# A hybrid decoder step on one core: keys and values of the last two heads as two pairs in seven products

## The chip, the cores and the metric

The kernel runs on one core of a Trainium2 chip. The metric is the device time of one execution in microseconds (us). Five engines work side by side, each through its own list of instructions in a fixed order: TensorE (PE in the profile; its weight loads are PEld), VectorE (DVE), ScalarE (ACT), GpSimd (POOL) and SyncE (SP), which here only issues DMAs. An instruction that waits for another engine holds up everything behind it in its own list. L269 is line 269 of the kernel.

## The reference, cut to what matters

One layer of a decoder: 16 meta tokens and 512 prompt tokens (causal) and 8 sequences of 4 new tokens each, which read a paged cache of 512 earlier positions (4 pages of 128 rows per sequence). Together 560 token columns; 8 heads of 128; model width 2048. Everything is float32.

```python
h = rmsnorm(x, g_pre)
q, k, v, ga, cb, cc, ch, gc, ma, mc = split(h @ w_in)
a = stick_breaking(q, k, v) * silu(ga)      # prompt: over its own rows; new tokens: pages, then their own rows
c = cb * causal_conv3(cc * ch) * silu(gc)
m = sigmoid(ma + b_ga) * (a @ w_pa) + sigmoid(mc + b_gc) * (c @ w_pc)
y = x + rmsnorm(m @ w_out, g_post)

def stick_breaking(q, k, v):
    z = q @ k.T * HEAD_DIM ** -0.5 + b_sb
    log_keep = where(mask, log_sigmoid(-z), 0)
    after = cumsum(log_keep, reverse) - log_keep
    return where(mask, exp(log_sigmoid(z) + after), 0) @ v
```

The outputs are the new rows of the prompt and of the 8 sequences, and the new keys, values and convolution rows.

## The kernel before, in words

**Products in split float32.** Each operand x is kept as a rounded part hi and the rest lo = x − hi. A product is three TensorE matmuls, hi·hi, hi·lo and lo·hi. The normalised input, turned so that its 2048 features lie in 16 blocks of 128 rows, stays in memory as `h_hi` and `h_lo`, 560 columns each, used as two halves of 280 (`HC`). Weights arrive from SP's DMA as pieces of 1024 rows by 128 columns (`w_load`, tile `raw`); `w_split` makes `whi` by a copy on ACT (L253) and `wlo` by a subtraction on DVE (L254).

**Two ways of making a projection.** `gemm` (L261 to L276, matmuls at L269) takes 128 columns of the weight at a time: 16 blocks × 3 matmuls × 2 halves = 96 matmuls of 280 columns. `pair` (L1044) takes 256 columns at once and cuts weight and input into 2 × 2 blocks; `seven` (L999) forms the result from seven block products instead of eight, each 8 × 3 = 24 matmuls (`product`, L994), 168 for two column tiles. For this, sums of input blocks T1, T2, T3 are needed (`t_hi0` to `t_lo2`, parts hi and lo), a fourth difference r1 that replaces one block of the input, and sums `s` of weight blocks.

**The stages.** First the normalisation, with the queries of heads 0 to 3 made as its columns come (`q_chunk`), and `q_proj` for these: scale, store, and a 128x32 transpose of the 32 decode columns per head. Then for each of heads 0 to 3 `head_now`: keys by `gemm` (`k_proj`), values by `gemm` (`v_proj`), the query of head 4 + h by `gemm`, and the stick-breaking attention of the prompt (`attend`; scores at L634, sums at L716, the product with the values at L728). Then `head_later` for heads 4 to 7: keys and values by `gemm`, turned by transposes (`natural`, L519 to L523), stored for later. Then all remaining projections by `pair`, then attention of heads 4 to 7, and the output products.

**The decode part** runs between these as a chain of small steps (`decode_steps`). A step of its first half takes one page of keys and makes 16 dot products of 128 elements on DVE (L795); there are 64 such pages. Calls of `dec_step` say how many steps stand at a place: in `head_now` and `head_later` 24 pages (`DEC1` = 6 units of 4) are worked, the other 40 by `dec_group`, one call per group of gate products.

**The block sums** T1 to T3 and r1 (lines 951 to 981) stand in the program behind `head_later`, two of eight feature blocks at a time, on 274 of the 280 columns: nine DVE operations, three ACT copies (L956) and three DVE subtractions (L957) for each of four rounds, and four more splits that put r1 into the input's block.

**The order.** Within an engine the order is a scheduler's, by priorities that follow the program's text, so work that stands later may fill gaps; an instruction put through `keep_in_program_order` (`pin`) stays in the order in which it was written against others so marked.

## Time and profile before

| what | us |
|---|---|
| median of 3 runs (lowest, highest) | 1575.22 (1573.78, 1578.06) |
| the profiled execution | 1577.82 |
| its span on the core | 1576.2 |
| PE busy in the span | 1561.8 |
| DVE busy | 1260.8 |
| ACT busy | 755.6 |

The mean granted TensorE clock of the profiled execution is 0.998 of full speed. The end of head 3's attention lies at 295 us of the span, the first matmul of a `pair` at 369.6.

In the profile a row of a group reads: line, engine, operation, output tile <- input tiles, count, busy time, mean time of one, idle time before and who ended it. A row of the timeline reads: start, duration, engine, line, operation, and in brackets the idle time just before on that engine and what ended it. Durations of pipelined instructions overlap, so what one costs when rows stand close is the distance of two starts. A window's row gives the stretch, its length, and the busy time of PE, PEld, DVE, ACT and POOL in it (instructions in brackets), then the granted TensorE clock, the DMA engines' share and GB/s.

### The profile page before, as it was taken

To read this page: it belongs to the slowest core of one execution; us is meant where nothing else is said; L and a number is where in the kernel's file an instruction comes from. 1 tells how busy PE (TensorE), PEld (TensorE's weight loads), DVE (VectorE), ACT (ScalarE), POOL (GpSimd) and SP (SyncE) were. 2 spreads that over 40 slices of the span, in tenths; PEclk is the share of its full clock that TensorE was granted. 3 is DMA by queue.
4 is the path that set the end of the run, shared out by engine and by line. 5 is a ranking of instruction groups with operands and counts; after the bars stand their busy time and mean duration, and the time that the engine had idled before them with its cause. 6 is when DMAs were issued, how large, how long until landed. Compare 5 with 4: busy or idle time off the path is not lost.

```text
span 1576.2 us, 32345 instructions
## 1 busy us (share of the span) xinstructions
PE 1561.8 (99%) x12172; PEld 1528.3 (97%) x12172; DVE 1260.8 (80%) x3567; ACT 755.6 (48%) x1345; POOL 236.3 (15%) x428
## 2 busy tenths in 40 slices
PE   9999999999999999999999999999999999999997
PEld 8999999999999999999999999898899999999997
DVE  6328999965799999999999996655678867877776
ACT  6335555434444443444444465444476734355563
POOL 1023333222011001011011113212100010000000
PEclk9999999999999999999999999999999999999999
DMA  8245655344563454545356547666596455433345
GB/s 250 73 143 175 178 165 178 117 125 130 170 189 113 144 153 143 149 135 162 106 173 187 157 143 224 185 207 219 166 292 188 140 186 167 153 107 95 101 140 189
DMA packets 300674, 252.77 MB, mean 160 GB/s; under 512 B 11521, under 2 KB 268613, under 8 KB 299701
## 3 DMA queue, kind: packets, MB, share of 16 engines
q1 hardware_dynamic: 272021, 160.45, 34.8%
q0 software_dynamic: 28368, 89.98, 17.2%
q8 instruction: 95, 1.56, 0.4%
q14 instruction: 62, 0.51, 0.1%
q10 hardware_dynamic: 128, 0.27, 0.1%
HBM read 217.95 MB, written 32.71 MB: 159 GB/s over the span
## 4 chain that ended last, share of the span: by engine, by line
PE 98%; DVE 1%; ACT 0%; issue 0%; DVEq 0%; ACTq 0%
PE mm L994 34%; PE mm L269 28%; PE o L994 25%; PE mm L334 2%; PE z L716 1%; PE o L728 1%; PE z L334 1%; PE tp L870 1%; PE z L634 1%; PE tp L519 0%; PE z L1332 0%; PE mm L187 0%; PE tp L169 0%; DVE x_n L1374 0%; PE z L227 0%; DVE hn L220 0%
## 5 line engine op out<-in xcount | busy, mean ns | idle before, releaser
L253 ACT CAST whi<-raw 128x1024 fp32r<-128x1024 f32 x247 | 259.3, 1051 | 323.1 <-PE mm L269 100.3
L254 DVE TENSOR_TENSOR wlo<-raw,whi 128x1024 fp32r<-128x1024 f32 x247 | 301.8, 1223 | 105.5 <-ACT whi L253 103.4
L994 PE MATMUL mm<-h_hi,whi 128*128 128x272 f32 (+1 forms) x1152 | 333.0, 289 | 0.0
L994 PE MATMUL mm<-h_lo,whi 128*128 128x272 f32 (+1 forms) x1152 | 332.7, 289 | 0.0
L994 PE MATMUL mm<-h_hi,wlo 128*128 128x272 f32 (+1 forms) x1152 | 331.7, 290 | 0.1
L994 PE MATMUL o<-t_hi,whi 128*128 128x272 f32 (+1 forms) x864 | 250.2, 290 | 0.0
L994 PE MATMUL o<-t_lo,whi 128*128 128x272 f32 (+1 forms) x864 | 249.9, 289 | 0.0
L994 PE MATMUL o<-t_hi,wlo 128*128 128x272 f32 (+1 forms) x864 | 249.8, 289 | 0.0
L795 DVE CUSTOM_DVE_ANT_0 junk<-kpage,qb 128x128 f32<-128x128 f32 x1024 | 245.3, 286 | 2.1 <-DMA qb<-q_scr 1.6
L994 PEld LDWEIGHTS mm<-h_hi,whi 128*128 128x128 f32 x1152 | 217.4, 189 | 6.7 <-ACT whi L253 3.4
L994 PEld LDWEIGHTS mm<-h_hi,wlo 128*128 128x128 f32 x1152 | 216.6, 189 | 1.3 <-DVE wlo L254 0.5
L994 PEld LDWEIGHTS mm<-h_lo,whi 128*128 128x128 f32 x1152 | 216.8, 188 | 0.1
L253 ACT CAST whi<-s 128x1024 fp32r<-128x1024 f32 x126 | 132.1, 1048 | 150.1 <-PE mm L994 54.2
L254 DVE TENSOR_TENSOR wlo<-s,whi 128x1024 fp32r<-128x1024 f32 x126 | 153.8, 1220 | 61.1 <-ACT whi L253 60.9
L269 PE MATMUL mm<-h_lo,whi 128*128 128x280 f32 (+1 forms) x640 | 187.6, 293 | 0.0
L269 PE MATMUL mm<-h_hi,wlo 128*128 128x280 f32 (+1 forms) x640 | 187.1, 293 | 0.0
L269 PE MATMUL mm<-h_hi,whi 128*128 128x280 f32 (+1 forms) x640 | 186.7, 292 | 0.0
L994 PEld LDWEIGHTS o<-t_hi,wlo 128*128 128x128 f32 x864 | 163.1, 189 | 0.7 <-DVE wlo L254 0.7
L994 PEld LDWEIGHTS o<-t_lo,whi 128*128 128x128 f32 x864 | 163.4, 189 | 0.0
L994 PEld LDWEIGHTS o<-t_hi,whi 128*128 128x128 f32 x864 | 163.0, 189 | 0.1
L269 PEld LDWEIGHTS mm<-h_lo,whi 128*128 128x128 f32 x640 | 120.3, 188 | 0.8
L269 PEld LDWEIGHTS mm<-h_hi,whi 128*128 128x128 f32 x640 | 120.5, 188 | 0.5
(462 smaller groups left out, 3166.7 us busy)
## 6 DMA issues: line engine op xcount, KB each, us to landing
raw<-in_w_in SPq DMA_DIRECT2D x192, 512.0 KB, 4.2
kpage<-in_cache_k POOLq DMA_DIRECT2D x64, 256.0 KB, 3.6
qb<-q_scr POOLq DMA_DIRECT2D x32, 512.0 KB, 5.7
vpage<-in_cache_v POOLq DMA_DIRECT2D x64, 256.0 KB, 5.9
raw<-in_w_out SPq DMA_DIRECT2D x32, 512.0 KB, 3.9
gate_scr<-g POOLq DMA_DIRECT2D x32, 272.0 KB, 3.3
gt<-gate_scr POOLq DMA_DIRECT2D x16, 544.0 KB, 4.6
raw<-in_w_pc SPq DMA_DIRECT2D x16, 512.0 KB, 4.5
```

Of the source, the lines that this page charges most:

```text
L253: act.copy(hi, x)
L254: low[0] = dve.tensor_sub(lo, x, hi.bitcast(F32))
L269: pe.matmul(o, lhsT=w, rhs=r[:, t0:t1], start=(k == 0 and n == 0), stop=(k == nk - 1 and n == 2))
L334: pin(pe.matmul(o, lhsT=l, rhs=r[:, k, t0:t1], start=(start and m == 0), stop=(stop and m == 2), skip_group_check=True))
L634: pe.matmul(zt[:m, c0:c0 + n], lhsT=l[:, s0:s0 + m], rhs=r[:, ts:ts + n], start=(c0 == 0 and i == 0), stop=(i == 2), skip_group_check=True)
L716: pe.matmul(o, lhsT=l, rhs=x, start=False, stop=(i == len(ops) - 1), skip_group_check=True)
L728: pe.matmul(ot[:, ts - NMETA:ts - NMETA + n], lhsT=l[:m, st, :], rhs=x[:m, c0:c0 + n], start=False, stop=(g == GROUPS[-1] and i == 2), ski ...
L795: dve.tensor_tensor_reduce(out=junk, in0=kt[:, h * P:(h + 1) * P], in1=qt[:, t, h * P:(h + 1) * P], scale=1.0, scalar=0.0, op0=ALU.mult, o ...
L870: pin(pe.matmul(po[32 * j:32 * (j + 1), :], lhsT=lhs, rhs=rhs, start=(pg == 0), stop=last and n >= len(vts) - 4, tile_position=(0, 32 * j) ...
L994: pe.matmul(o, lhsT=l[:, k, :], rhs=r, start=(start and k == 0 and m == 0), stop=(stop and k == 7 and m == 2), skip_group_check=True)
```

## The change

It has three parts.

1. **Keys and values of heads 6 and 7** are made by `pair`, keys of both heads in one pair and values in another (`later_pair`). Heads 4 and 5 stay with `gemm`: four column tiles, now written as a loop in which the block sums stand by hand between the tiles (`STEPS`). The first pair's weight pieces and its first sum `s` are loaded and formed within the last of these four tiles (`ready`).
2. **The block sums** cover all 280 columns and are written in two steps of two feature blocks each: `t_sums` (six DVE operations) and `t_parts` (two DVE operations, three ACT copies, three DVE subtractions). They are pinned, and so are the `wlo` of the four tiles. The copies of 16 and 32 rows in `natural` move from DVE to ACT for heads 4 and 5.
3. **The first decode queries.** The decode columns of heads 0 to 3 are turned by one 128x128 transpose, copied once and stored by four DMAs together, ahead of the loads of the small tables. `PAGES` sets the steps: one page before head 0, then 19 in heads 0 to 3, so that 20 pages are worked there (`DEC1` = 5) and 44 by `dec_group`. The decode queries of heads 6 and 7 are read back from memory for their `z_new`.

```diff
-DEC1 = 6
+DEC1 = 5
+SOLO = 6
-    def w_split(x):
+    def w_split(x, pin=lambda ins: ins):
...
-        low[0] = dve.tensor_sub(lo, x, hi.bitcast(F32))
+        low[0] = pin(dve.tensor_sub(lo, x, hi.bitcast(F32)))
...
-    def natural(raw, nat, nat_s):
+    def natural(raw, nat, nat_s, copy=dve.tensor_copy):
...
+        if h < FIRST:
+            act.activation(qs_all[:, h, :], ob[:, PQ - HQ:], AF.Copy, scale=SCALE)
         pool.dma_start(qt_scr[h][:, q0:], qr[:, q0:])
+        if h < FIRST:
+            return
...
+    PAGES = ((2, 2, 2, 1), (1, 1, 2, 1), (1, 1, 1, 1), (1, 1, 1, 0))
...
         khi, klo = k_split(np_, k_proj(h))
-        dec_step(1 if h else 0, "part")
-        vhi, vlo = v_proj(h, np_)
-        dec_step(1, "part")
+        dec_step(PAGES[h][0], "part")
+        vhi, vlo = v_split(np_, v_proj(h))
+        dec_step(PAGES[h][1], "part")
         q_proj(NOW + h)
-        dec_step(2, "part")
+        dec_step(PAGES[h][2], "part")
         ot = next(attend(np_, h, khi, klo, vhi, vlo, *q_split(np_, qr)))
-        dec_step(2, "part")
-        at = np_.tile([P, PQ], F32, name="at", bufs=1)
+        dec_step(PAGES[h][3], "part")
+        at = hp.tile([P, TQ], F32, name="qr", bufs=2)[:, 0:PQ]
...
-    def head_later(h):
-        pool.dma_start(k_scr[h], k_proj(h))
-        dec_step(2, "part")
-        v_proj(h)
-        dec_step(2, "part")
+    def later_pair(c, h, qs=None, ready=None):
+
+        raws = [hp2.tile([P, T], F32, name="raw", bufs=2) for _ in range(2)]
+        seen = []
+        for m, half, b in pair(c + h * P, HC, ready):
+            act.copy(raws[m][:, NMETA + half * HQ:NMETA + (half + 1) * HQ], b[:, HM:])
+            act.copy(raws[m][:, half * HM:(half + 1) * HM], b[:, :HM])
...
-        if n <= 25:
+        if n <= 27:
...
-            dec_step(2 if n in (26, 28) else 1)
+            dec_step(2 if n <= 30 else 1)
+    for h in range(FIRST):
+        q_proj(h)
+    pt = t_ps()
+    pe.transpose(out=pt[:, 0:P], in_=qs_all[:, 0:FIRST, :].rearrange("p h t -> p (h t)"), identity=ident)
+    qn = hp.tile([P, P], F32, name="qn4", bufs=1)
+    act.copy(qn, pt[:, 0:P])
+    for h in range(FIRST):
+        pool.dma_start(q_scr[:, h * P:(h + 1) * P], qn[h * TS:(h + 1) * TS])
...
+    dec_step(1, "part")
...
-    for h in range(NOW, H):
-        head_later(h)
...
+        def whole(out, c, *ij):
+            pin(dve.tensor_add(out, part(h_f, c, *ij), part(l_f, c, *ij)))
+        def t_sums(c):
+
+            x, y = held[c] = [tsp.tile([P, 2, HC], F32, name=n) for n in "xy"]
+            r = part(r1, c)
+            whole(y, c, 0, 0)
+            whole(r, c, 0, 1)
+            pin(dve.tensor_sub(r, y, r))
+            whole(x, c, 1, 1)
+            pin(dve.tensor_add(x, r, x))
+            pin(dve.tensor_sub(y, y, x))
+        def t_parts(c):
+
+            x, y = held.pop(c)
+            t_split(part(t_hi[0], c), part(t_lo[0], c), x)
+            z = tsp.tile([P, 2, HC], F32, name="z", bufs=1)
+            whole(z, c, 1, 0)
+            t_split(part(t_hi[1], c), part(t_lo[1], c), y)
+            pin(dve.tensor_sub(z, z, x))
+            t_split(part(t_hi[2], c), part(t_lo[2], c), z)
+        tiles = [c + h * P for h in range(NOW, SOLO) for c in (GATE_K, GATE_V)]
...
+        units = {(0, u): unit(0, u) for u in range(2)}
+        STEPS = (((t_sums, 0),), ((t_sums, 2), (t_parts, 0)), ((t_parts, 2), (t_sums, 4), (t_parts, 4)),
+                 ((t_sums, 6), (t_parts, 6)))
+        for i in range(len(tiles)):
+            h = NOW + i // 2
+            if i:
+                units[i, 1] = unit(i, 1, pin)
+            o = gemm([units[i, u] for u in range(2)], h_rhs, ALL)
+            if i + 1 == len(tiles):
+                first_ws = blocks_of(win, GATE_K + SOLO * P)
+            for step, c in STEPS[i]:
+                step(c)
+            if i + 1 < len(tiles):
+                units[i + 1, 0] = unit(i + 1, 0, pin)
+            else:
+                pin(dve.tensor_add(first_sum, first_ws[1], first_ws[2]))
+                for c in range(0, 8, 2):
+                    t_split(blk(h_hi, 0, 1)[:, c:c + 2], blk(h_lo, 0, 1)[:, c:c + 2], r1[:, c:c + 2])
+            raw = raw_of(o)
+            if i % 2 == 0:
+                k_store(h, raw)
+                k_out(hp, h, raw, qs_all[:, h, :], act.copy)
+            else:
+                v_store(h, v_out(hp, h, raw, act.copy))
...
-    def seven(ws, n, rb, rt, s, tmp, sums=None):
+    def seven(ws, n, rb, rt, s, tmp, sums=None, summed=False):
...
+        later_pair(GATE_K, SOLO, qs, (first_ws, first_sum))
+        later_pair(GATE_V, SOLO)
```

Behind the pairs the program is as before, but for the tile `after`, which is made a little later from another pool.

Three places show how the change moves the rows. Line numbers of the kernel before and of the changed one differ by a few: the `gemm` matmul is L269 before and L270 now, the values' product of `attend` L728 and L722, `natural`'s transposes L519 to L523 and L501 to L505, the casts of T L956 and L992, the subtractions behind them L957 and L993.

The first place is TensorE at the end of head 3's attention (its output is `o_3998` before, `o_3939` now). Before, `mm_4471` is the keys of head 5 in `gemm`, and `tp_4442`, `tp_4448` are the transposes of head 4's values:

```order
L728 MATMUL o_3998<-hiA_4049,vhi_3652 128x512
L519 MATMUL tp_4442<-ident_73,raw_4435 128x128 x4
L269 MATMUL mm_4471<-h_hi_89,wlo_4468 128x280
...
L728 MATMUL o_3998<-loA_4050,vhi_3652 128x512
L728 MATMUL o_3998<-hiA_4049,vlo_3653 128x512
L269 MATMUL mm_4471<-h_lo_90,whi_4467 128x280
...
L269 MATMUL mm_4472<-h_hi_89,whi_4461 128x280
L522 MATMUL tp_4448<-ident_73,raw_4435 16x128
L523 MATMUL tp_4448<-ident_73,raw_4435 32x128
```

Now, with `tp_4308` and `tp_4314` the transposes of head 4's values, `mm_4331` the keys of head 5 and `mm_4492` its values:

```order
L722 MATMUL o_3939<-hiA_3990,vhi_3640 128x512
L722 MATMUL o_3939<-loA_3991,vhi_3640 128x512
L722 MATMUL o_3939<-hiA_3990,vlo_3641 128x512
L501 MATMUL tp_4308<-ident_73,raw_4301 128x128 x4
L270 MATMUL mm_4492<-h_hi_89,whi_4457 128x280
L270 MATMUL mm_4492<-h_lo_90,whi_4457 128x280
L504 MATMUL tp_4314<-ident_73,raw_4301 16x128
L505 MATMUL tp_4314<-ident_73,raw_4301 32x128
L270 MATMUL mm_4331<-h_hi_89,wlo_4298 128x280
L270 MATMUL mm_4331<-h_hi_89,whi_4297 128x280
```

Between the four large transposes of head 4's values and the two small ones, which use the same buffer, 25 matmuls stood; now two stand there.

The second place is ScalarE at the same point. `at_4142` before and `qr_3997` now is the copy of head 3's attention output. Before:

```order
L520 COPY nat_4440<-tp_4442 128x512
L745 COPY at_4142<-o_3998 128x512
L579 COPY raw_4569<-mm_4471 128x272
L579 COPY raw_4569<-mm_4471 128x8
L253 CAST whi_4602<-raw_4600 128x1024
...
L956 CAST t_hi0_5269<-x_5285 128x548
```

Now:

```order
L741 COPY qr_3997<-o_3939 128x512
L992 CAST t_hi0_4005<-x_4135 128x560
L992 CAST t_hi1_4010<-y_4136 128x560
L992 CAST t_hi0_4005<-x_4278 128x560
L992 CAST t_hi1_4010<-y_4279 128x560
L502 COPY nat_4306<-tp_4308 128x512
L506 COPY nat_4306<-tp_4314 16x128
L992 CAST t_hi2_4015<-z_4288 128x560
```

The copy `nat` that empties the buffer of head 4's large transposes stood ahead of the attention output's copy; now it stands behind that copy and four casts of the block sums.

The third place is VectorE behind the last operation of head 3's attention (`loA`). Now, with `wlo_4298` and `wlo_4328` the low parts of the weights of head 5's keys:

```order
L491 TENSOR_TENSOR loA_3991<-eA_3987,hiA_3990 128x512
L993 TENSOR_TENSOR t_lo0_4006<-x_4135,t_hi0_4005 128x560
L1007 TENSOR_TENSOR z_4288<-h_hi_89,h_lo_90 128x560
L993 TENSOR_TENSOR t_lo1_4011<-y_4136,t_hi1_4010 128x560
L1027 TENSOR_TENSOR z_4288<-z_4288,x_4135 128x560
L993 TENSOR_TENSOR t_lo2_4016<-z_4288,t_hi2_4015 128x560
L255 TENSOR_TENSOR wlo_4298<-raw_4295,whi_4297 128x1024
L255 TENSOR_TENSOR wlo_4328<-raw_4325,whi_4327 128x1024
```

Before, the block sums stood among the weights of later heads, mostly one at a time:

```order
L254 TENSOR_TENSOR wlo_4603<-raw_4600,whi_4602 128x1024
L968 TENSOR_TENSOR r1_5284<-r1_5284,h_lo_90 128x548
L969 TENSOR_TENSOR x_5285<-r1_5284,h_hi_89 128x548
L969 TENSOR_TENSOR x_5302<-r1_5284,h_hi_89 128x548
L254 TENSOR_TENSOR wlo_4731<-raw_4728,whi_4730 128x1024
L970 TENSOR_TENSOR x_5285<-x_5285,h_lo_90 128x548
```

The subtraction that makes the weights' low part for the next tile now has the five rows of `t_parts` ahead of it; before, it had one or two rows of the sums between it and the next. From `t_lo0_4006` to the low part of the first pair's sum `s`, 36 rows of 560 elements and 8 of 1024 stand on VectorE.

More of the change, by code (lines that the diff above doesn't have):

```diff
@@ L523, in natural @@
         pe.transpose(out=pt[0:TS, P:2 * P], in_=raw[:, TP:T], identity=ident)
-        dve.tensor_copy(nat[0:16, 4, :], pt[0:16, 0:P])
-        dve.tensor_copy(nat_s, pt[0:TS, P:2 * P])
+        copy(nat[0:16, 4, :], pt[0:16, 0:P])
+        copy(nat_s, pt[0:TS, P:2 * P])
     BLK = {}
@@ L933, in hybrid_step_kernel @@
     for h in range(NOW):
-        q_proj(h)
-    for h in range(NOW):
         head_now(h)
     nctx.close()
-    for h in range(NOW, H):
-        head_later(h)
     dec_step(64, "part")
@@ L947, in hybrid_step_kernel, with blocks_of @@
         ttp = tctx.enter_context(tc.tile_pool(name=f"tt{i}", bufs=1))
-        t_hi.append(ttp.tile([P, 8, HU], F32R, name=f"t_hi{i}"))
-        t_lo.append(ttp.tile([P, 8, HU], F32R, name=f"t_lo{i}"))
+        t_hi.append(ttp.tile([P, 8, HC], F32R, name=f"t_hi{i}"))
+        t_lo.append(ttp.tile([P, 8, HC], F32R, name=f"t_lo{i}"))
+    def blocks_of(src, c):
+        c1, c2, k1, k2 = slice(c, c + P), slice(c + P, c + 2 * P), slice(0, 1024), slice(1024, 2048)
+        return [w_load(src[k, m]) for k, m in ((k1, c1), (k1, c2), (k2, c2), (k2, c1))]
@@ L978, in hybrid_step_kernel, with part @@
-        for c in range(0, 8, 2):
-            t_split(blk(h_hi, 0, 1)[:, c:c + 2], blk(h_lo, 0, 1)[:, c:c + 2], r1[:, c:c + 2])
+        r1 = tsp.tile([P, 8, HC], F32, name="r1", bufs=1)
+        first_sum = sp2.tile([P, 8, P], F32, name="s")
+        held = {}
+        def part(x, c, *ij):
+            return (blk(x, *ij) if ij else x)[:, c:c + 2]
+        def whole(out, c, *ij):
[9 more added lines that the diff above has]
+            pin(dve.tensor_sub(y, y, x))
@@ L1011, in seven @@
         product(x, w_split(w11), rb(0, 0), True, False)
-        with behind(last):
-            dve.tensor_add(s, w21, w22)
+        if not summed:
+            with behind(last):
+                dve.tensor_add(s, w21, w22)
         product(q, w_split(s), rb(0, 1), True, False)
@@ L1037, in seven, with pair @@
         yield 1, 0, y
-    def blocks_of(src, c):
-        c1, c2, k1, k2 = slice(c, c + P), slice(c + P, c + 2 * P), slice(0, 1024), slice(1024, 2048)
-        return [w_load(src[k, m]) for k, m in ((k1, c1), (k1, c2), (k2, c2), (k2, c1))]
-    def pair(c, n):
+    def pair(c, n, ready=None):
         hs = [(HC - n, HC), (T - n, T)]
@@ L1051, in rt @@
         def rt(i):
-            return lambda k: (t_hi[i][:, k, HU - n:HU], t_lo[i][:, k, HU - n:HU])
-        ws = blocks_of(win, c)
-        s = sp2.tile([P, 8, P], F32, name="s")
-        yield from seven(ws, n, rb, rt, s, lambda name: sp2.tile([P, HU], F32, name=name)[:, :n])
-    gctx, uctx = ExitStack(), ExitStack()
-    sp2 = gctx.enter_context(tc.tile_pool(name="sums", bufs=1))
+            return lambda k: (t_hi[i][:, k, HC - n:], t_lo[i][:, k, HC - n:])
+        ws, s = ready or (blocks_of(win, c), sp2.tile([P, 8, P], F32, name="s"))
+        yield from seven(ws, n, rb, rt, s, lambda name: sp2.tile([P, HC], F32, name=name)[:, :n], summed=ready is not None)
+    with tc.tile_pool(name="heads2", bufs=1) as hp2:
+        qs = hp2.tile([P, H - SOLO, TS], F32, name="qs")
+        for h in range(SOLO, H):
+            pool.dma_start(qs[:, h - SOLO, :], qt_scr[h][:, PQ:TQ])
+        later_pair(GATE_K, SOLO, qs, (first_ws, first_sum))
+        later_pair(GATE_V, SOLO)
     gp = gctx.enter_context(tc.tile_pool(name="gates", bufs=2))
@@ L1163, in hybrid_step_kernel @@
             if j + w == 14:
-                after = hl[0].tile([P, P], F32, name="after")
-                dve.tensor_scalar_add(after, neg_u.bitcast(F32), 1.0)
                 loaded = head_loads(NOW, hl[0])
@@ L1170, in hybrid_step_kernel @@
     hs0 = hlctx.enter_context(tc.tile_pool(name="split0", bufs=1, side="right"))
+    after = hs0.tile([P, P], F32, name="after")
+    dve.tensor_scalar_add(after, neg_u.bitcast(F32), 1.0)
     def head_split(pl, x):
```

108 lines of the change are left out of this document (53 added, 55 removed).

## The prediction

> **What bounds the kernel now.** I read the page's first part, then the chain of waits, then TensorE's waits.
>
> ```profile
> PE 1561.8 (99%) x12172; PEld 1528.3 (97%) x12172; DVE 1260.8 (80%) x3567; ACT 755.6 (48%) x1345; POOL 236.3 (15%) x428
> PE 98%; DVE 1%; ACT 0%; issue 0%; DVEq 0%; ACTq 0%
> PE o L227 <- DVE hn L220: 2.0, 2, 1.3
> PE tp L169 <- DVE neg_one L114: 1.4, 1, 1.4
> PE z L227 <- DVE hn L220: 0.5, 1, 0.5
> ```
>
> TensorE is busy for 99% of the span and is 98% of the chain. The three waits, 3.9 us together, are the only ones that the view of TensorE's waits gives, and they belong to the normalisation. So a matmul less is time less, and any wait that the change brings to TensorE is time more: there is no slack of TensorE that could absorb it. The windows by stage (length, then PE, PEld, DVE, ACT and POOL busy) show how near the other engines are:
>
> ```profile
> 42.00:93.00 51.00, 51.00 (x392) 50.23 (x391) 14.25 (x24) 15.41 (x31) 8.21 (x15) 1.00 0.32 96
> 93.00:271.00 178.00, 178.00 (x1367) 173.61 (x1366) 152.39 (x799) 93.82 (x190) 59.19 (x110) 1.00 0.56 168
> 271.00:370.00 99.00, 99.00 (x766) 97.07 (x766) 75.17 (x216) 40.27 (x82) 23.33 (x43) 1.00 0.39 116
> 455.00:945.00 490.00, 489.94 (x3860) 487.70 (x3860) 474.13 (x1591) 225.16 (x336) 54.42 (x90) 1.00 0.50 149
> 945.00:1164.00 219.00, 219.00 (x1735) 202.53 (x1734) 133.89 (x152) 101.53 (x145) 46.61 (x85) 1.00 0.66 208
> ```
>
> From 93 us to 271 us (heads 0 to 2 and most of 3) VectorE is at 86%, and TensorE still never waits. From 271 to 370, where the keys and values of heads 4 to 7 and all block sums lie, it is at 76%: the sums cost TensorE nothing, because eight column tiles of 96 matmuls cover them.
>
> **What is removed.** Four column tiles of 96 matmuls become two pairs of 168: 384 − 336 = 48 matmuls of 280 columns less. One costs, from the chain:
>
> ```profile
> 168.99 8.99 PE mm L269 x70
> 369.63 3.03 PE mm L994 x24
> 92.77 0.27 PE L552 MATMUL tp<-ident,qr 128*32 128x128 f32 x1
> 92.80 0.38 PE L269 MATMUL mm<-h_lo,whi 128*128 128x280 f32 x1
> 93.02 0.29 PE L269 MATMUL mm<-h_hi,wlo 128*128 128x280 f32 x1
> ```
>
> 8.99 / 70 = 0.128 us (a `product` of 272 to 280 columns: 3.03 / 24 = 0.126). 48 × 0.1285 = **6.2 us**. Four turned queries become one: the turn sets the next matmul off by 0.03 and that one lasts 0.09 longer than usual (0.22 to its successor), 0.12 each, so three fewer give 0.35. Together **−6.5 us**. The Trainium skill ("TensorE: Matmul & The Clock Gate", section "Wait — 56ns, not 53.3ns?") gives a warm matmul its columns at 2.4 GHz and 2.5 ns, 119 ns for 280, which would make the 48 worth 5.7 us; the row here measures 128 ns, and it decides.
>
> **What the cover loses.** The block sums now have four column tiles to hide behind, and the second product of the first pair has its weights' low part on VectorE behind all of them. I work this out from s, the start of head 3's last attention matmul.
>
> ```profile
> 295.35 0.40 PE L728 MATMUL o<-hiA,vlo 128*128 128x512 f32 x1
> 295.78 0.59 ACT L745 COPY at<-o 128x512 f32<-128x512 f32 x1 [1.29 <-PE o L728]
> 308.01 0.59 ACT L520 COPY nat<-tp 128x512 f32<-128x512 f32 x1 [3.14 <-PE tp L519]
> 308.49 0.28 ACT L587 ACTIVATE z_new<-z,bsb 32x32 f32<-32x32 f32 x1
> 308.68 1.18 ACT L956 CAST t_hi<-x 128x548 fp32r<-128x548 f32 x2
> 323.93 0.66 ACT L956 CAST t_hi<-x 128x548 fp32r<-128x548 f32 x1
> 269.69 0.40 PE L716 MATMUL z<-hiA,neg_u 128*128 128x512 f32 x1
> 269.92 0.29 PE L269 MATMUL mm<-h_lo,whi 128*128 128x280 f32 x1
> 275.77 0.60 PE L519 MATMUL tp<-ident,raw 128*128 128x128 f32 x4
> 276.13 0.38 PE L269 MATMUL mm<-h_hi,whi 128*128 128x280 f32 x1
> ```
>
> *First stall.* The small transposes of head 4's values share a buffer with the large ones and wait for its copy `nat`. In the new order that copy stands on ScalarE behind the attention output's copy and four casts. The output's copy starts at s + 0.43 (295.35 to 295.78) and holds ScalarE for 0.48 (308.01 to 308.49); casts follow each other at 1.18 − 0.66 = 0.52, call it 0.53 for 560 columns; `nat` takes 0.59 and its signal 0.04: 0.43 + 0.48 + 4 × 0.53 + 0.59 + 0.04 = 3.66. TensorE has until then the last attention matmul (269.69 to 269.92, 0.23), four transposes (0.36) and two matmuls (0.26): 0.85. It waits **2.8 us**. Before, 25 matmuls (3.2 us) stood at that place.
>
> *Second stall.* Directly behind these transposes stands the first matmul with the low weights of head 5's keys. That subtraction is pinned on VectorE behind the five rows of `t_parts`.
>
> ```profile
> 309.34 0.73 DVE L957 TENSOR_TENSOR t_lo<-x,t_hi 128x548 fp32r<-128x548 f32 x1 [0.60 <-ACT t_hi L956]
> 309.99 0.72 DVE L973 TENSOR_TENSOR y<-y,h_lo 128x548 f32<-128x548 f32 x1
> 310.63 0.72 DVE L957 TENSOR_TENSOR t_lo<-x,t_hi 128x548 fp32r<-128x548 f32 x1
> 336.07 0.73 DVE L957 TENSOR_TENSOR t_lo<-x,t_hi 128x548 fp32r<-128x548 f32 x1 [0.86 <-ACT t_hi L956]
> 301.93 1.21 DVE L254 TENSOR_TENSOR wlo<-raw,whi 128x1024 fp32r<-128x1024 f32 x1
> 303.06 0.71 DVE L968 TENSOR_TENSOR r<-r,h_lo 128x548 f32<-128x548 f32 x1
> 122.67 0.43 DVE L486 TENSOR_SCALAR loA<-eA 128x512 f32<-128x512 f32 x1 [1.38 <-ACT eA L481]
> 123.14 0.69 DVE L487 TENSOR_TENSOR loA<-eA,loA 128x512 f32<-128x512 f32 x1
> ```
>
> Short rows follow each other at 0.64 (309.99 to 310.63), a long one holds VectorE for 1.13 (301.93 to 303.06). The fifth row, t_lo2, needs the cast of z, which stands behind `nat` and the small copy, thus behind the first stall: cast from about s + 4.2 to 4.9, t_lo2 0.64, the long row 1.25 to its end, about s + 6.8. TensorE is there at 3.66 + 0.24 = 3.9. It waits **2.9 us**.
>
> *The whole stretch.* From t_lo0 to the low part of the pair's sum s, which the third matmul of the pair's second product needs, VectorE has 36 short and 8 long rows (the order above). It starts at s + 0.43 + 0.48 + 0.66 + 0.03 = s + 1.6; 36 × 0.64 + 7 × 1.13 + 1.25 = 32.2; in each of four `t_parts` it waits for the last cast, 0.86 as in the row at 336.07, 3.4 together: s + 37.2. TensorE needs 214 matmuls × 0.1285 = 27.5, the attention matmul 0.23 and some 2.6 of transposes: s + 30.3. So it loses at least **6.9 us**, of which the two stalls are 5.7 and the rest falls at the start of values 5 and of the pair. Some rows need the row right ahead (r = y − r, x = r + x, y − x, z − x): there the successor starts only after the full duration and 0.04 (122.67 + 0.43, then 123.14). With 12 such rows at 0.12 it is 8.3. With every row at its full 0.72 or 1.22 (40.7) it is 10.4. I take **8.7**, nearest to the dependent count with a little for the signals between engines; bounds 6.9 to 10.4. Below 6.9 it could come only if VectorE's rows ran closer than the row at 309.99 shows.
>
> **Early decode steps.** By the new order 25 dot products lie inside head 0's sums where 6 lay before.
>
> ```profile
> 125.89 0.29 DVE L795 CUSTOM_DVE_ANT_0 junk<-kpage,qb 128x128 f32<-128x128 f32 x1
> 126.10 0.29 DVE L795 CUSTOM_DVE_ANT_0 junk<-kpage,qb 128x128 f32<-128x128 f32 x1
> ```
>
> At 0.21 each, 19 more are 4.0 us of VectorE ahead of what TensorE needs. Heads 1 to 3 have had as many before and TensorE waited for none, so most of it is covered by the matmuls of the next query: bounds 0 to 4.0, I take **0.6**. Four stores and the tables' loads change places in POOL's queue in a stretch in which POOL is busy 8.21 of 51 us (the window from 42 us); what waits for them (the bias in `z_new`, the first page) stands behind head 0's keys, a dozen us of matmuls. I cost them at nothing; a late bias would hold ScalarE's next weight copy and TensorE behind it.
>
> **At nothing.** The four pages that move to `dec_group` are 4 × 16 × 0.21 = 13.4 us of VectorE. Calls per group are unchanged up to the 25th group, so the stretch from 455 us, where VectorE is at 474.13 of 490, keeps its density; the pages land where it is busy 133.89 of 219. Without that room each would cost up to 3.4. The weights of the pairs are as many pieces as those of four tiles, so SP's queue is as long; the two small reloads of queries are wanted only at the end of a pair.
>
> **The sum**, against the profiled execution (1577.82 with a span of 1576.2): −6.5 + 8.7 + 0.6 = **+2.8 us**, 1580.6 for such an execution. The median of the runs shown is 1575.22, 2.6 lower, so there: **1578.0 us**. What a measurement of this kernel can tell from no change is about 0.3%, 4.7 us: the forecast is no change, on the slow side.
>
> **Rivals.**
>
> *The saving stays.* The waits are absorbed and 6.5 us, or nearly, remain: 1568.7. For it: 271 to 370 us had the same sums at 75.17 of 99 and no wait. Against: that took eight tiles, and the ledger leaves 37 us of VectorE beside 30 of TensorE. Chance 0.15.
>
> *Head 0 waits too.* The sums of head 0 stand, by the new order, behind 51 dot products in all, and TensorE pays the whole 4.0: −6.5 + 8.7 + 4.0 = +6.2, 1581.4, slower. It decides once VectorE reaches head 0's sums later than TensorE has run through the next query's 96 matmuls (12.3 us). For it: VectorE is at 86% there. Against: heads 1 to 3. Chance 0.20.
>
> *The clock drops.* After two stalls with 0.24 us of work between them TensorE may be granted half its clock. At the start of the span ten wide matmuls run slow:
>
> ```profile
> 1.36 4.63 PE tp L169 x10
> ```
>
> 0.46 each against 0.23 at 269.69, and full speed after 4.6 us; that again costs half, 2.3 us: +5.1, 1580.3. Chance 0.10. The Trainium skill ("TensorE: Matmul & The Clock Gate", section "What's actually happening") lets the clock halve after an idle window of about 3.4 us, in windows that run freely; the stalls of 2.8 and 2.9 would each stay under it, and by that rule the drop mostly does not come.
>
> **How the numbers follow.** The forecast has 0.55; its own range is 1574.5 to 1581 (stretch 6.9 to 10.4 and head 0 at 0 to 1 give 1575.6 to 1580.1, and 1 us to each side for the scatter of the median). The range reaches to the head 0 rival with the stretch at 10.4 in part, 1584, and toward the saving to 1571, which leaves out most of the first rival and a little at the top: **1571.0 to 1584.0**. Slower by over 0.3% is above 1579.9: 0.12 of the forecast, 0.18 of head 0, 0.05 of the clock, **0.35**. Faster, under 1570.5: **0.13**. Within: **0.52**.
>
> **What would show it.** TensorE's waits should name `nat` (2.8) and `wlo` (2.9) behind head 3's attention, then shorter ones up to the pair, 7 to 10 us in all, in a stretch where VectorE is close to full. The first matmul of the keys' pair of heads 6 and 7 and all later stages should keep their old lengths. No waits there, waits in the gate products, a granted clock below 1.00, or a head 0 with more than 1 us of waits would each make a term wrong.

## The result and the profile after

The changed kernel takes 1585.55 us (median of 4 runs, 1585.03 to 1586.16) against 1574.57 us of the kernel before beside it (4 runs, 1573.78 to 1578.06): a ratio of 1.0067, 95% interval 1.0054 to 1.0079. It is 0.67% or 11 us slower. The prediction had 1578.0 us, no change, and a range that ends at 1584.0.

The first part of the changed kernel's page:

```profile
span 1583.4 us, 32270 instructions
PE 1554.8 (98%) x12121; PEld 1520.3 (96%) x12121; DVE 1269.7 (80%) x3569; ACT 763.1 (48%) x1366; POOL 245.0 (15%) x430
```

TensorE is busy 7.0 us less than before (1561.8), and the span is 7.2 us longer. The 7.0 is not the 48 matmuls alone: 5.3 of it lies ahead of the first `gemm` matmul, where executions differ anyway, and matmuls at half clock, seen below, count as busy for longer. The view of TensorE's waits (who waits, for whom, us in total, times, longest) has new rows besides those of the normalisation:

```profile
PE mm L270 <- DVE wlo L255: 4.5, 2, 2.8
PE tp L504 <- ACT nat L502: 3.1, 2, 2.7
PE z L710 <- ACT hiA L490: 1.8, 1, 1.8
PE z L574 <- ACT raw L564: 1.0, 1, 1.0
PE mm L1073 <- DVE wlo L255: 0.7, 1, 0.7
PE tp L876 <- DMA vpage<-in_cache_v: 0.7, 1, 0.7
```

And the windows by stage (columns as in the prediction):

```profile
93.00:271.00 178.00, 174.20 (x1320) 169.56 (x1319) 149.71 (x790) 92.04 (x179) 63.45 (x103) 0.99 0.48 152
271.00:370.00 99.00, 91.34 (x674) 88.22 (x673) 68.07 (x89) 46.35 (x95) 22.08 (x41) 0.97 0.37 111
455.00:945.00 490.00, 489.92 (x3874) 488.18 (x3872) 474.01 (x1634) 216.28 (x322) 55.04 (x95) 1.00 0.51 153
```

The loss lies in the first two windows: TensorE is idle for 3.8 us in heads 0 to 3 and for 7.7 us in the stretch after them, and the granted clock is under 1.00 in both. The third window stands as before, although four pages more now lie behind it.

Spans of single executions are not directly comparable here: the first `gemm` matmul starts at 78.4 us in the profile of before and at 74.7 us in that of after, in a part that the change does not touch (e10 below, with the changed beginning, starts there at 78.15). So I measure from that matmul. To the first matmul of the convolution's first pair it takes 291.1 us before and 301.0 us after, **+9.95**; from there to the last product of `seven` 1183.9 and 1184.4, and in every experiment 1183.0 to 1184.5. Nearly all of the change lies in the first piece. I cut it again at s, the start of head 3's last attention matmul, and take 0.1285 us off for each `gemm` or `seven` matmul in between, since orders differ in how many stand on which side. What is left, "net", is the other matmuls, every wait and what half clock costs:

| kernel | heads 0 to 3, net | s to third matmul of the pair's second product, net | first gemm to convolution |
|---|---|---|---|
| before | 39.5 | – | 291.1 |
| after | 44.3 | 13.8 | 301.0 |
| e1 late steps | 39.7 | 13.7 | 296.4 |
| e2 registers behind | 43.7 | 13.7 | 300.3 |
| e3 units ahead | 47.5 | 12.8 | 304.3 |
| e4 no pair | 46.6 | – | 298.6 |
| e5 unpinned, late | 39.4 | 1.6 | 286.6 |
| e6 one pair, late | 38.9 | 3.8 | 286.6 |
| e7 lows on POOL, late | 42.7 | 16.3 | 303.2 |
| e8 wait filled, late | 39.6 | 12.2 | 294.9 |
| e9 unpinned, early | 47.4 | 1.7 | 293.1 |
| e10 four query tiles | 38.7 | 12.7 | 294.3 |
| e11 e10 and unpinned | 39.0 | 1.7 | 284.8 |
| e12 e5, four query tiles | 39.2 | 1.6 | 286.4 |

The 12.2 us of e8 hold 6.1 us of matmuls that it adds. Without any wait the second column would still hold up to 3 us, mostly of transposes; the unpinned kernels have fewer of them there (8 large ones, 12 in the changed kernel) and reach 1.6. Waits that come behind the third matmul of the second product show in the last column alone.

**Behind head 3's attention** the trace has the two stalls where the prediction put them. TensorE's timeline of after:

```profile
292.17 0.40 PE L722 MATMUL o<-hiA,vlo 128*128 128x512 f32 x1
292.98 0.29 PE L270 MATMUL mm<-h_lo,whi 128*128 128x280 f32 x1
295.96 0.28 PE L504 MATMUL tp<-ident,raw 128*16 128x128 f32 x1 [2.69 <-ACT nat L502]
299.16 0.60 PE L270 MATMUL mm<-h_hi,wlo 128*128 128x280 f32 x1 [2.81 <-DVE wlo L255]
299.56 0.44 PE L270 MATMUL mm<-h_hi,whi 128*128 128x280 f32 x1
```

They last 2.7 and 2.8 us; 2.8 and 2.9 were forecast. The last row shows something else: a matmul of 0.44 us instead of 0.29. Windows of 1 us, TensorE alone (length, busy, matmuls, granted clock, DMA share, GB/s):

```profile
297.00:298.00 1.00, 0.00 (x0) 1.00 0.48 147
298.00:299.00 1.00, 0.00 (x0) 0.71 0.74 217
299.00:300.00 1.00, 0.84 (x3) 0.50 0.64 178
304.00:305.00 1.00, 1.00 (x6) 0.50 0.14 40
305.00:306.00 1.00, 1.00 (x9) 0.88 0.00 0
306.00:307.00 1.00, 1.00 (x10) 1.00 0.00 0
```

From 298.4 to 305.2 us the granted clock is 0.50, and TensorE does 6 matmuls a us instead of 10. From 299.16 on it works without a break there, so this costs about 3.0 us. (The texts written before the runs put the waits behind head 3's attention at 8.4 us. TensorE is idle there for 7.7; the other 0.7 is the wait for `vpage`, at 1023 us.)

**In head 0** the first dot products, moved ahead of it, come late. POOL's, VectorE's and TensorE's rows:

```profile
93.78 1.99 POOL L944 DMA_DIRECT2D q_scr<-qn  x4 [2.94 <-ACT stc L963]
100.37 2.17 POOL L792 DMA_DIRECT2D qb<-q_scr  x3 [4.61 <-issue]
```

```profile
104.45 0.29 DVE L801 CUSTOM_DVE_ANT_0 junk<-kpage,qb 128x128 f32<-128x128 f32 x1 [8.28 <-DMA qb<-q_scr]
105.30 1.22 DVE L255 TENSOR_TENSOR wlo<-raw,whi 128x1024 fp32r<-128x1024 f32 x1
```

```profile
106.58 0.39 PE L270 MATMUL mm<-h_hi,wlo 128*128 128x272 f32 x1 [1.73 <-DVE wlo L255]
```

VectorE stands for 8.28 us before its first dot product, whose queries are loaded only at 100.37. The low weights of head 0's values are queued behind four of these dot products, and TensorE waits 1.73 us for them. The clock falls here too, from 107.3 to 110.7 us, which costs 1.7 us. In head 1 the wait for `hiA` (1.8) follows.

### The profile page after: what moved, and what is told of

Same layout as the page of the kernel before. It is cut to its first block, busy times and chain, and to the rows that moved or that the text cites. A ratio compares the mean times of both kernels' runs of the same rounds, so it can differ in the third digit from the quotient of the medians.

```text
span 1583.4 us, 32270 instructions
## 1 busy us (share of the span) xinstructions
PE 1554.8 (98%) x12121; PEld 1520.3 (96%) x12121; DVE 1269.7 (80%) x3569; ACT 763.1 (48%) x1366; POOL 245.0 (15%) x430
## 4 chain that ended last, share of the span: by engine, by line
PE 90%; DVE 3%; issue 2%; DMA 2%; ACT 1%; POOL 1%; POOLq 1%; DVEq 0%; ACTq 0%
PE mm L1073 34%; PE o L1073 25%; PE mm L270 21%; PE mm L335 1%; PE z L335 1%; PE z L710 1%; PE tp L876 1%; PE o L722 1%; PE z L628 1%; DMA qb<-q_scr 1%; POOLq L776 1%; DMA vpage<-in_cache_v 1%; DVE junk L801 1%; DVE wlo L255 1%; PE z L1410 0%
## 5 line engine op out<-in xcount | busy, mean ns | idle before, releaser
L1073 PE MATMUL mm<-h_hi,whi 128*128 128x272 f32 (+2 forms) x1216 | 352.0, 290 | 0.0
L1073 PE MATMUL mm<-h_hi,wlo 128*128 128x272 f32 (+2 forms) x1216 | 350.8, 290 | 0.8 <-DVE wlo L255 0.7
L1073 PE MATMUL mm<-h_lo,whi 128*128 128x272 f32 (+2 forms) x1216 | 351.3, 289 | 0.0
L1073 PE MATMUL o<-t_hi,wlo 128*128 128x272 f32 (+2 forms) x912 | 264.2, 290 | 0.0
L1073 PE MATMUL o<-t_hi,whi 128*128 128x272 f32 (+2 forms) x912 | 263.9, 289 | 0.0
L1073 PE MATMUL o<-t_lo,whi 128*128 128x272 f32 (+2 forms) x912 | 263.1, 288 | 0.0
L1073 PEld LDWEIGHTS mm<-h_hi,whi 128*128 128x128 f32 x1216 | 229.6, 189 | 5.2 <-issue 2.5
L1073 PEld LDWEIGHTS mm<-h_hi,wlo 128*128 128x128 f32 x1216 | 228.6, 189 | 2.0 <-DVE wlo L255 1.8
L1073 PEld LDWEIGHTS mm<-h_lo,whi 128*128 128x128 f32 x1216 | 228.9, 188 | 1.0 <-issue 0.8
L270 PE MATMUL mm<-h_hi,wlo 128*128 128x280 f32 (+1 forms) x512 | 151.5, 296 | 4.5 <-DVE wlo L255 4.5
L270 PE MATMUL mm<-h_lo,whi 128*128 128x280 f32 (+1 forms) x512 | 151.4, 296 | 0.0
L270 PE MATMUL mm<-h_hi,whi 128*128 128x280 f32 (+1 forms) x512 | 151.4, 296 | 0.0
L270 PEld LDWEIGHTS mm<-h_hi,wlo 128*128 128x128 f32 x512 | 98.1, 192 | 5.3 <-DVE wlo L255 5.0
L270 PE MATMUL mm<-c_hl,whi 128*128 128x272 f32 x512 | 100.8, 289 | 0.0
```

Of the source, the lines that this page charges most:

```text
L270: pe.matmul(o, lhsT=w, rhs=r[:, t0:t1], start=(k == 0 and n == 0), stop=(k == nk - 1 and n == 2))
L1073: pe.matmul(o, lhsT=l[:, k, :], rhs=r, start=(start and k == 0 and m == 0), stop=(stop and k == 7 and m == 2), skip_group_check=True)
```

## The experiments

All were run beside the kernel before. "Late" means that e1's edit is in.

**e1: the decode steps at their old places.** Still 20 pages, none ahead of head 0.

```diff
-    PAGES = ((2, 2, 2, 1), (1, 1, 2, 1), (1, 1, 1, 1), (1, 1, 1, 0))
+    PAGES = ((0, 1, 2, 2), (1, 1, 2, 2), (1, 1, 2, 1), (1, 1, 1, 1))
-    dec_step(1, "part")
```

> The changed kernel (1585.55 us), with the decode steps put back to the places of the kernel before: no page ahead of head 0, and PAGES = ((0, 1, 2, 2), (1, 1, 2, 2), (1, 1, 2, 1), (1, 1, 1, 1)), still 20 pages. Theory 'late first queries': in the changed kernel the first dot products wait for their queries, and the low weights of head 0's values stand behind them; with that gone TensorE's waits at 105 us (1.7) and in head 1 (1.8 and 0.3) and the half-clock spell from 107 us (1.7) go: -5.5, about 1580.0. Rival 'VectorE is too full': the same dot products only wait elsewhere in heads 0 to 3, at most -2, 1583.5 or more. Both expect the waits behind head 3's attention (8.4 in all) and the half clock from 298 us unchanged.

1580.24 us, ratio to before 1.003 [1.002, 1.004]: 5.3 us less than the changed kernel. Heads 0 to 3 are back at 39.7 net, and the window from 93 us is full again:

```profile
93.00:271.00 178.00, 178.00 (x1366) 173.88 (x1365) 155.94 (x798) 94.41 (x182) 56.72 (x104) 1.00 0.51 156
```

So the early steps cost 5 us. The loss behind head 3 stays; TensorE is idle for 8.7 us there, most of it in one piece, and the half clock behind it costs about 2.7:

```profile
PE mm L270 <- DVE wlo L255: 6.6, 1, 6.6
```

**e2: page registers behind the first query loads.** In the order of POOL's queue eight reads of page numbers into registers stand between the queries' stores and their load. The timeline does not show such reads; they fill the 4.61 us marked "issue" above, 0.59 each. The chain of work shows them (start, duration):

```profile
97.38 0.29 POOLq L776
97.67 0.07 issue
97.75 0.15 POOLq L776
97.97 0.28 POOLq L776
```

Twelve more stand ahead of the stores, from 85.1 us on. The edit moves them all behind the load.

```diff
+    first_qb = []
...
+            with tc.issue_after(first_qb[-1].ins) if first_qb and i >= NPG else nullcontext():
                 page_reg[i] = pool.value_load(pt_i[0:1, i:i + 1], min_val=0, max_val=NPOOL - 1)
```

(`first_qb` holds the two query loads of the first unit; the lines that fill it are left out.)

> The changed kernel with one thing moved on POOL's queue: the page numbers of later pages are read into registers behind the first three loads of decode queries, not ahead of them. Theory 'late first queries' with its cause on POOL's queue (4.6 us without a visible instruction between the stores of the queries and the load that reads them): the load goes out about 4.6 us earlier, the wait at 105 us and the half-clock spell behind it go, -3.4, about 1582.1; head 1's wait of 1.8 may stay. Rival 'VectorE is too full', or the transfer itself is what is late: no change, 1585.5.

1585.16 us, ratio 1.0053 [1.0034, 1.0072]: nothing gained in the end, so the rival's number. But the mechanism was right as far as head 0 goes: the load goes out at 96.02 us, 5.2 us earlier counted from the first `gemm` matmul. Of this, 4.6 come from the stores, which start that much earlier; between the stores and the load still lie 4.00 us, now a wait for the stores to land. So it was the twelve reads ahead of the stores that counted, and the eight behind them cost 0.6. No wait for `wlo` is left at 105 us, and TensorE is 3.5 us ahead of the changed kernel after 240 `gemm` matmuls. After 680 of them, in head 1, 2.9 of the 3.5 are lost. There VectorE stops once more:

```profile
158.91 0.29 DVE L805 CUSTOM_DVE_ANT_0 junk<-kpage,qb 128x128 f32<-128x128 f32 x1 [2.67 <-DMA qb<-q_scr]
```

and the wait for `hiA` of 1.8 us, which had left the clock alone in the changed kernel, now halves it. One delay hid the next.

**e3: the next tile's first weights ahead of the block sums.**

```diff
+            if i + 1 < len(tiles):
+                units[i + 1, 0] = unit(i + 1, 0, pin)
             for step, c in STEPS[i]:
                 step(c)
-            if i + 1 < len(tiles):
-                units[i + 1, 0] = unit(i + 1, 0, pin)
-            else:
+            if i + 1 == len(tiles):
```

> The changed kernel with the first half of the next tile's weights split ahead of the block sums' step, not behind it. Theory 'throughput' (the ledger of the prediction: between the end of head 3's attention and the pair's second product VectorE has 36 short and now 7 long rows, TensorE 205 matmuls instead of 215): 36.1 + 1.4 against 29.2, so the waits add up to about 8 us as before, only elsewhere; 1584 to 1586, or 3 lower if they come in pieces so short that the clock stays. Rival 'order' (the wait comes only from the low weights standing behind five rows): the second stall (3.0) and the half-clock spell (3.0) go, about 1579.5.

1589.02 us, ratio 1.0078 [1.0059, 1.0096]. In the stretch the throughput theory holds: the second stall is gone from its place, but the waits for `wlo` come back later and larger, and the stretch takes 12.8 net instead of 13.8, about the one long row (1.13) that VectorE had less (of the 5.7 us below, 2.0 lie in head 0):

```profile
PE mm L270 <- DVE wlo L255: 5.7, 3, 3.0
PE mm L1073 <- DVE wlo L255: 2.6, 1, 2.6
```

The whole time missed its expectation by 3 us, through heads 0 to 3 (47.5 instead of 44.3), where the edit moves nothing up to head 2. There the clock did not fall at 107 us, TensorE ran ahead of VectorE, waited more often in heads 0 and 1, and the clock fell at 182 us. e4 and e9, with the same beginning, show the same. In these three the first `gemm` matmul starts 0.6 to 0.9 us later than in the changed kernel, and the wait in head 0, just as long or longer, is split by a line of the grid on which the clock changes (last section): 1.65, 1.18 and 1.22 us of idle time fall into one window, 1.73 in the changed kernel. That is why the clock stays there. Why they then lose more in head 1 is open.

**e4: no pair.** Eight `gemm` tiles, one step of block sums behind each.

```diff
-SOLO = 6
+SOLO = 8
-        STEPS = (((t_sums, 0),), ((t_sums, 2), (t_parts, 0)), ((t_parts, 2), (t_sums, 4), (t_parts, 4)),
-                 ((t_sums, 6), (t_parts, 6)))
+        STEPS = (((t_sums, 0),), ((t_sums, 2),), ((t_parts, 0),), ((t_parts, 2),), ((t_sums, 4),), ((t_parts, 4),),
+                 ((t_sums, 6),), ((t_parts, 6),))
...
```

The calls of `later_pair` and the first pair's early sum go too.

> The changed kernel without its pairs: keys and values of heads 6 and 7 by gemm in the same loop, so eight column tiles, the block sums one step per tile. 48 matmuls more cost 6.2; if the short cover is what makes the waits, all 8.4 us of waits and the half clock from 298 us (3.0) go: 1585.5 + 6.2 - 11.4 = about 1580.3, and what stays above the kernel before are the early decode steps. Rival: the block sums as written (pinned, 560 columns) stall TensorE themselves: waits stay and the time is 1588 or more.

1581.47 us, ratio 1.0037 [1.0024, 1.005], near the 1580.3 of the cover theory. Pinned rows as such stall nothing when there are eight tiles to cover them:

```profile
271.00:370.00 99.00, 99.00 (x765) 96.94 (x765) 52.79 (x71) 41.95 (x93) 24.37 (x44) 1.00 0.37 113
```

**e5: the block sums unpinned** (late). The scheduler may now put them where their users need them.

```diff
-        pin(dve.tensor_sub(lo, x, hi.bitcast(F32)))
+        dve.tensor_sub(lo, x, hi.bitcast(F32))
...
-            pin(dve.tensor_add(out, part(h_f, c, *ij), part(l_f, c, *ij)))
+            dve.tensor_add(out, part(h_f, c, *ij), part(l_f, c, *ij))
...
-                units[i, 1] = unit(i, 1, pin)
+                units[i, 1] = unit(i, 1)
```

(and so for the other rows of `t_sums` and `t_parts`, `units[i + 1, 0]` and the first sum).

> The kernel of e1 (late first steps, 1580.24 us) with the block sums and the weights of the four tiles no longer pinned: the scheduler now puts only 21 short and 2 long rows ahead of the low part of the pair's first sum, and the last parts of T1 and T2 behind it, since the pair needs them only in its later products. Theory 'written order' (the waits come from forcing all of T through VectorE ahead of the pair): the 8.4 us of waits fall to 2 or 3 and the half clock (3.1) goes, about 1571.5. Rival 'throughput' (VectorE has too many rows for four tiles of cover, whatever their order): the waits only come later, in the pair, 1579 to 1581.

1570.32 us, ratio 0.9964 [0.995, 0.9978]: faster than both kernels, with both pairs. The stretch falls from 13.7 to 1.6 net, and the way to the convolution by 9.8 us; the difference went into waits that now lie behind the stretch and transposes that lie outside it. Besides the normalisation's waits and one of 0.2, TensorE has two left, inside the pair:

```profile
PE o L1072 <- ACT whi L254: 1.7, 1, 1.7
PE mm L1072 <- ACT whi L254: 0.4, 1, 0.4
```

The seven products need the sums one after the other: the second r1, the third T1, the fifth T2, the seventh T3. The written order put all of them ahead of the second product's weights; the free one puts 21 short and 2 long rows there instead of 36 and 8.

**e6: one pair** (late). The values of heads 6 and 7 by `gemm`, six tiles.

```diff
         tiles = [c + h * P for h in range(NOW, SOLO) for c in (GATE_K, GATE_V)]
+        tiles += [GATE_V + h * P for h in range(SOLO, H)]
...
+        STEPS = (((t_sums, 0),), ((t_sums, 2),), ((t_parts, 0),), ((t_parts, 2), (t_sums, 4)),
+                 ((t_parts, 4), (t_sums, 6)), ((t_parts, 6),))
...
-        later_pair(GATE_V, SOLO)
```

> The kernel of e1 with the values of heads 6 and 7 back in gemm, six column tiles, one pair (keys), the block sums spread over the six tiles. Theory 'cover': 24 matmuls more cost 3.1, the waits behind head 3's attention (8.4) and the half clock (3.1) go: 1580.2 + 3.1 - 11.5 = about 1571.8, below the kernel before. Rival: the pinned rows stall TensorE whatever the cover: 1580 or more.

1572.44 us, ratio 0.998 [0.997, 0.9989], as the cover theory says (1571.8). So the pinned order may stand if there is work to hide it: two tiles more cost 3.1 us and remove the waits but one of 0.8.

**e7: sums ahead, low parts on POOL** (late). All four `t_sums` ahead of the attention's end (four buffers for x and y; z is formed in x; the first pair's sum is made in the pair), e3's edit, and on POOL the low part of T2 and of r1.

```diff
-            t_split(part(t_hi[1], c), part(t_lo[1], c), y)
+            t_split(part(t_hi[1], c), part(t_lo[1], c), y, pool)
...
-                    t_split(blk(h_hi, 0, 1)[:, c:c + 2], blk(h_lo, 0, 1)[:, c:c + 2], r1[:, c:c + 2])
+                    t_split(blk(h_hi, 0, 1)[:, c:c + 2], blk(h_lo, 0, 1)[:, c:c + 2], r1[:, c:c + 2], pool)
```

> The kernel of e1 with both pairs, and VectorE relieved between head 3's attention and the pair: all four rounds of sums ahead of the attention's end, eight low parts (T1's middle one and r1's) on POOL, the next weights ahead of the block sums. VectorE then has 16 short and 7 long rows there (10.2 + 8.0 + 1.6 + returns 3.4 = 23.2) against TensorE's 165 matmuls and transposes (24). Theory 'throughput': waits of at most 2, no half clock, about 1570. Rival: POOL takes longer for such a row than VectorE or slows it, and the pair waits for POOL: 1577 or more.

1588.28 us, ratio 1.0082 [1.0064, 1.01], the rival. The durations were not as expected. POOL's row, then VectorE's:

```profile
299.39 5.03 POOL L992 TENSOR_TENSOR t_lo<-y,t_hi 128x560 fp32r<-128x560 f32 x3 [0.35 <-ACT t_hi L991]
```

```profile
299.55 1.81 DVE L1022 TENSOR_TENSOR x<-h_hi,x 128x560 f32<-128x560 f32 x1
301.39 1.80 DVE L1023 TENSOR_TENSOR x<-x,h_lo 128x560 f32<-128x560 f32 x1
303.92 1.10 DVE L992 TENSOR_TENSOR t_lo<-x,t_hi 128x560 fp32r<-128x560 f32 x1 [0.72 <-ACT t_hi L991]
307.98 0.74 DVE L1022 TENSOR_TENSOR x<-h_hi,x 128x560 f32<-128x560 f32 x1
330.54 1.23 DVE L1087 TENSOR_TENSOR s<-raw 128x1024 f32<-128x1024 f32 x1 [10.05 <-POOL h_lo L992]
```

A row on POOL takes 1.7 us, and while it runs the same row on VectorE takes 1.81 instead of 0.74. Three rows on VectorE became 2.5 us longer in this way, and the three that POOL took over are worth some 2.0 there: the help costs more than it saves. The Trainium skill names the contention ("GPSIMD Engine Reference", section "8. Key points": POOL shares its memory interfaces with VectorE and contends with instructions that have two inputs there), and the trace agrees. TensorE waited 8.6 us in one piece. The slower rows are a part of the 8 us that e7 loses against e1: VectorE also stood 10.05 us for POOL's low parts of r1 (last row above), and heads 0 to 3 lost 3.0 more than in e1, with waits of 1.8 us and the clock at half from 293.2 us on. These parts were not tested apart.

**e8: the wait filled** (late). 26 useless matmuls of 512 columns behind head 3's attention.

```diff
+    with tc.issue_after(last_o[0].ins):
+        fill = z_ps()
+        for _ in range(26):
+            pin(pe.matmul(fill, lhsT=neg_one, rhs=neg_one.unsqueeze(1).broadcast_to([P, 4, P]), start=True, stop=True))
```

(`last_o` is the last matmul of `attend`.)

> The kernel of e1 with 26 useless matmuls of 512 columns (about 0.23 us each, 6.0 together) on TensorE right behind head 3's last attention matmul, where it waits 6.6 us. Theory 'idle halves the clock': the matmuls fit into the wait, the granted clock stays at 1.00 from 293 us, and the 3.1 us lost at half clock come back: about 1577.1 though TensorE does more. Rival 'the half clock has another cause or costs nothing there': 1580.2 or more.

1579.61 us, ratio 1.0026 [1.0016, 1.0036]; e1 had 1580.24. The fillers do fit into the wait, and the clock stays at 1.00 all the way:

```profile
288.00 6.08 PE L973 MATMUL z<-neg_one 128*128 128x512 f32 x26
294.74 0.40 PE L270 MATMUL mm<-h_hi,wlo 128*128 128x280 f32 x1 [0.48 <-DVE wlo L255]
```

TensorE alone from 293 to 301 us, in e1 and then in e8:

```profile
293.00:301.00 8.00, 6.14 (x29) 0.57 0.46 133
293.00:301.00 8.00, 7.52 (x55) 1.00 0.46 133
```

So it is the idle time that halves the clock. But of e1's 2.7 us at half clock only 0.6 come back in the median, and the two intervals overlap; in the traces it is 1.4 from s to the pair's second product (40.9 to 39.5). TensorE reaches VectorE's next late row earlier and waits there. Within this stretch, which VectorE bounds, about half of what the half clock costs stands in the place of waits.

**e9: unpinned alone**, e5's edit without e1's.

> The changed kernel (1585.55 us) with the block sums and the four tiles' weights unpinned as in e5, but with the early decode steps kept. Theory 'two separate losses': the free order gives the same 9.9 us as between e1 (1580.24) and e5 (1570.32), and heads 0 to 3 keep their 5 to 7 us of waits: 1575 to 1578, about the kernel before. Rival: the early steps cost only because of the pinned rows behind them: 1570 to 1572.

1576.3 us, ratio 1.0004 [0.9994, 1.0013]: 9.25 less than the changed kernel (9.9 from e1 to e5). In the medians the two losses are separate. In the traces heads 0 to 3 keep theirs and take e3's course (47.4 net, 3.1 more than the changed kernel), and the stretch behind them gains more (12.1 net).

**e10: four buffers for the decode queries**, on e2.

```diff
-                        qt = d1.tile([P, 2, 512], F32, name="qb", bufs=3)
+                        qt = d1.tile([P, 2, 512], F32, name="qb", bufs=4)
```

> The kernel of e2 (page registers behind the first query loads, 1585.16 us) with four buffers for the decode queries, not three. In e2 head 0's 3.5 us came back and were lost again in head 1, where VectorE stands 2.6 us before a dot product whose queries were loaded only when a third buffer came free. Theory 'query tiles': with a fourth buffer that load goes out earlier, head 1's waits go too, and most of what e1 gained (5.3) is gained with the early steps in place: about 1580.5. Rival 'too many dot products ahead of head 1's sums': the queries are there, VectorE is still late, 1584 or more.

1578.81 us, ratio 1.0016 [1.0007, 1.0026]: 6.4 less than e2, more than expected. Heads 0 to 3 take 38.7 net, less than before, with the same dot products at the same places. So it was not the number of dot products: each unit takes two query tiles of three, the second waits for a buffer that a dot product must free first, and the transfer (6.7 us in the chain of waits of after) then stops VectorE. Between 93 and 180 us VectorE waits for queries for 10.9 us in the changed kernel, 8.9 in e2 and 3.7 in e10. A fourth buffer without e2's edit was not run.

**e11: both cures** (the edits of e2, e10 and e5's unpinning, early steps in place), and **e12**: e5 with e10's four query tiles.

> Both cures together, with the changed kernel's early steps in place: page registers behind the first query loads and four query buffers (e10, 1578.81), block sums and tile weights unpinned (e5, worth 9.9). Theory 'two separate losses, both order and buffers': 1578.8 - 9.9 = about 1569, the 48 matmuls' full 6.2 below the kernel before. Rival: what the free order gains needs heads 0 to 3 as in e5: 1572 or more.

> The kernel of e5 (late first steps, unpinned, 1570.32) with four query buffers. Theory: with late steps no dot product waits for its queries in a way that reaches TensorE, so a fourth buffer changes nothing: 1570.3 within 1. Rival: the buffers are short in the later heads too, 1568.5 or less.

e11: 1569.89 us, ratio 0.9962 [0.9948, 0.9975]; e12: 1571.46 us, 0.9975 [0.9966, 0.9984]. e11 is the best version together with e5 (1570.32; their intervals cover each other); it has the shortest way to the convolution, 284.8 against 291.1 before, and 1.2 us of waits left in the pair. e12 is 1.1 us above e5 where at most 1 was expected, and their intervals overlap: with late steps a fourth buffer is of no use.

## Why the prediction was wrong, step by step

**The saving (−6.5)** is right: e11, with 1.2 us of waits left, is 6.3 us shorter from the first `gemm` matmul to the convolution than before.

**The stretch behind head 3 (+8.7, bounds 6.9 to 10.4)** is right in place and mechanism and too small. The two stalls came as forecast (2.7 and 2.8). From s to the third matmul of the second product it takes 41.25 us in the trace against the 30.3 of work, 10.9 lost: 7.7 in waits and about 3.0 at half clock. VectorE's rows between, the first, the one with the longest wait and the last:

```profile
293.78 0.74 DVE L993 TENSOR_TENSOR t_lo<-x,t_hi 128x560 fp32r<-128x560 f32 x1 [4.12 <-ACT t_hi L992]
324.29 0.74 DVE L993 TENSOR_TENSOR t_lo<-y,t_hi 128x560 fp32r<-128x560 f32 x1 [2.07 <-ACT t_hi L992]
332.15 1.22 DVE L255 TENSOR_TENSOR wlo<-s,whi 128x1024 fp32r<-128x1024 f32 x1
```

They are the 36 short and 8 long ones, they begin at s + 1.6 as forecast, and without waits they take 33.8 us (32.2, or 33.6 with the dependent rows, in the ledger). The term that was too small is VectorE's waits for the casts, put at 0.86 in each of four `t_parts`, 3.4 together: they are 5.8. The longest stands behind a copy on ScalarE that waits for TensorE. In e1 they are 5.4, and in e8, the same order at full clock, 4.1, with the stretch 1.4 shorter. e3 shows that the count of rows sets the loss and not one row's place. What the ledger took as given, that all 36 rows have to be through first, is the written order's doing: e5 drops it and has 2.1 us of waits left.

**Early decode steps, "I take 0.6"**, is the step that failed. Heads 0 to 3 lose 4.8 net (44.3 against 39.5), and e1 gets 5.3 back. I priced dot products by VectorE's time at 0.21 us each and asked whether matmuls cover it. VectorE's time was not the matter (e10 has all of them and loses nothing); the queries were late. The prediction looked past POOL's queue with "I cost them at nothing". Twenty register reads of 0.59 us, those that e2 moves, stand in it ahead of the queries' first load, and three buffers hold the queries where four are needed (e10); VectorE then stands, with the weights' low parts queued behind it. The prediction's own signs of error, a head 0 with more than 1 us of waits and a granted clock below 1.00, both came. The size came near the rival's 4.0, but by luck: its reason, VectorE's time for the dot products, is not what e10 shows.

**The clock** I gave a chance of 0.10 and 2.3 us, on the ground that each stall is under 3.4 us. It fell for three windows of 3.41 us, one in head 0 (1.7 us) and two behind head 3 (3.0), although no single wait was longer than 2.8. Its cost is partly not its own, as e8 shows.

**The sum.** −6.5 + 10.9 + 4.8 = +9.2; measured +9.95 to the convolution in the traces. Counted directly, the waits (3.8 and 7.7) and the half clock (1.7 and 3.0) make 16.2, less 6.5 is +9.7. From the convolution to the end the traces differ by another 0.9, no more than the experiments among themselves; the medians differ by 11.0. The forecast's stretch and two rivals, each with a chance, all came at once. They do not exclude each other, so they should have been added: 8.7 + 4.0 + 2.3 − 6.5 = +8.5, nearer to the result, though the 4.0 had the wrong reason.

**At nothing:** the four pages moved to `dec_group` cost nothing, as said (the window from 455 us, and 1184 us from the convolution on in both).

## What to carry to other kernels

Count for each engine the rows that stand between two fixed points of the new order, and ask of each whether the next user needs it there: a hand-written order that forces all of a sum through an engine ahead of its first use can cost more than the work it prepares saves. When a step is moved ahead, follow its data back to the load and to the queue that issues it, with buffers and register reads, before pricing its compute. Rivals that can happen together are terms of a sum.
